# Last state-space unit turned on the vector engine, gated unit first in the fill, modulation loads in the SP queue, a weight tile with a place of its own

## The chip, the cores and the metric

The kernel runs on one core of a Trainium2 chip. The metric is device microseconds (us) from the start to the end of one execution; the median of the runs is compared. The core has five engines that run side by side, each through its own instructions in their order: TensorE (PE in the rows; PEld is its weight load), VectorE (DVE), ScalarE (ACT), GpSimd (POOL) and SyncE (SP). DMA transfers are started by an instruction in the stream of SP or of ACT; such an instruction can wait, for a free buffer for instance, and what stands behind it on that engine then waits too.

## The reference

An encoder trunk with two residual layers, width 1024, 512 tokens, one sequence, all in fp32. The change lies in the first layer, in its mixer:

```python
u = rms_norm(h, norm_w[layer, 0]) * (1.0 + sc1) + sh1
z = u @ hyb_w_in[e]                      # split: state-space part, queries, keys, values
y_s5 = s5_mixer(z_s5, ...)               # 512 wide, forward and backward complex scan
y_att = axial_gqa(z_q, z_k, z_v, ...)    # 512 wide, 8 query heads, 2 key/value heads
mix = jnp.concatenate([y_s5, y_att], axis=-1) @ hyb_w_out[e]
h = h + g1 * mix
# inside s5_mixer, behind the scans:
g = jax.nn.gelu(y)
out = g * jax.nn.sigmoid(g @ glu_w + glu_b)      # the gated unit
```

`sh1, sc1, g1, sh2, sc2, g2` are the modulation: `silu(c) @ ada_w[layer] + ada_b[layer]`, a 1024 x 6144 product for one row. The norm behind the mixer uses `sc2` and `sh2`.

## The kernel before

Matrix products are made in three passes for fp32 accuracy: each operand is split into a high part `hi` (a rounded copy, from ACT or POOL) and a low part `lo` (the difference, from DVE), and `hi*hi + hi*lo + lo*hi` is summed in PSUM. So a weight tile needs a load (`wr`), a cast (`wh`, ACT, line L522) and a subtraction (`wl`, DVE, line L523) before PE can use it whole.

The first layer's mixer runs in this order in the trace. From about 100 us on, the loop in `hybrid` walks eight state-space units (four channel groups, two directions) and lets attention steps run between them. A unit is: a product with the input matrices (L445), a rotation by DVE (L450 to L452) that makes the complex recurrence a real one, two pairs of scans on DVE (L459), and `s5_turn`, which turns the states back: four multiplies (L470 to L473) on the engine that the list `POST` names, two additions on DVE (L475, L476), and the output product on PE (L483). A channel group is finished by `s5_out` (L496 to L503), whose result is a tile of `gts`.

Behind the loop come three things that are interleaved by a scheduler, which orders each engine's instructions by its own estimate, PE's alone being in the order of the code (`manual_schedule`):

- `gelu2` for the four tiles of `gts` (L1109 to L1112), and their split (POOL L520, DVE L523, tile names `actb`);
- the last attention steps (scores L1021 and L1022, row maximum L1024 on DVE, exponential L1028 on ACT, transposes L1036, their copies `pts` L1038, values L1045), and between them the pieces of `fill`. A piece is six matmuls of 128x512: two output tiles, one input tile, three passes. `fill` makes the gated unit (weights `gluw`, inputs `actb`; its exit is a tanh L1143, a product L1144 and a split L1147, L1148 into tiles `ys5`) and half of the output projection: `pa` and `pb`, two tiles each, with weights `wa`, `wb` for the attention half and `ws` for the state-space half;
- `ada_half` for four halves of `sc2` and `sh2`: eight loads of 256 KB each (tile `araw`, line L693), a multiply-add of each into `aacc` on DVE (L695, L700), a transposed copy and a sum (L706, L708), four tiny matmuls (L710, tile `po`).

```python
behind = lambda: self.tc.issue_after(self.scan.ins)
```

keeps `gelu2` and `fill` behind the last scan in the scheduler's order. `hybrid_out` then calls `boundary`, which takes `pa` and `pb` out (L1372 in the profile's numbers) and multiplies the second half of the output projection with four more weight tiles (loads in the SP queue, four buffers of their own).

The tile pools say how many buffers a tile name has: `araw` four, raw weights `wr` three, cast weights `wh`, `wl` two in that stretch; `wa` has its own place in the pool `op`, `wb` has not. A load waits until its buffer's last reader is done.

Of the kernel before, what the change touches and what calls it, by code (L numbers as in the profile page):

```python
# [12 lines left out]
F32R = mybir.dt.float32r  # L13
I32 = mybir.dt.int32
AF = mybir.ActivationFunctionType
# [4 lines left out]
P = 128  # L20
# [40 lines left out]
class Kern:  # L61
# [54 lines left out]
    def setup(self, cols, consts):  # L116
        nc, ctx = self.nc, self.ctx
        G = nc.gpsimd
        self.POST = [(G, G)] * 8
# [258 lines left out]
    def s5_phase(self, sp, pg, d, eng):  # L378


        A = self.nc.scalar
        e = self.tl(sp, "s5e", [P, 12, 128], bufs=2).rearrange("p (i x) j -> p i x j", i=3)
        m4 = self.tl(sp, "s5m4t", [P, 4, 128], bufs=2)
        place = lambda t: t.rearrange("p (a b) j -> p b a j", b=2)
        pairs = lambda t: t.rearrange("p (a b) j -> p a b j", b=2)
        er, ei, ni = (e[:, i, :, d:d + 127] for i in range(3))
        c, s = (t[:, d, pg % 2 * 4:pg % 2 * 4 + 4] for t in self.tabs)
        A.copy(place(er[:, :, 63:127]), pairs(c))
        A.copy(place(ei[:, :, 63:127]), pairs(s))
        A.copy(place(er[:, :, 0:63]), pairs(c[:, :, 63:0:-1]))  # L390
        A.mul(place(ei[:, :, 0:63]), pairs(s[:, :, 63:0:-1]), -1.0)
        A.mul(ni, ei, -1.0)
        x0 = d * 16 + pg * 4
        A.copy(place(m4[:, :, d:d + 127]), pairs(self.s5["m4"][:, x0:x0 + 4].unsqueeze(2).to_broadcast([P, 4, 127])))
        end = slice(127 * (1 - d), 127 * (1 - d) + 1)
        self.nc.gpsimd.memset(m4[:, :, end], 0.0)
        self.nc.gpsimd.memset(e.rearrange("p i x j -> p (i x) j")[:, :, end], 0.0)
        return e, m4
# [28 lines left out]
    def s5_states(self, sp, pg, d, e, m4, ut):  # L427
# [9 lines left out]
        for x1 in range(2):  # L437
# [15 lines left out]
            for i, v in enumerate((vr, vi)):  # L453
# [5 lines left out]
                self.scan = V.tensor_tensor_scan(*z, 0.0, op0=ALU.mult, op1=ALU.add)  # L459
            yield vr, vi  # L460

    def s5_turn(self, pg, d, e, vr, vi, eng):
# [13 lines left out]
        V.tensor_tensor(vr[:, dst], vr[:, dst], vi[:, dst], op=ALU.add)  # L476
# [68 lines left out]
    def wtile(self, src, pool=None):  # L545
# [4 lines left out]
        hi, lo = (self.tl(pool or self.wp, t, [P, self.WC], F32R, bufs=1 if pool else self.WH)[:, 0:n] for t in ("wh", "wl"))  # L550
# [135 lines left out]
    def ada_half(self, aw, l, q, half, tag, eng=None, acc=None, raws=None, trn=None):  # L686
# [4 lines left out]
        for k in range(8):  # L691
            raw = raws()
            self.adma = nc.scalar.dma_start(raw, aw[l, k * 128:(k + 1) * 128, c0:c0 + 512])  # L693
# [420 lines left out]
    def fill(self, op, gts, yatt, acts, gluw, wout, outs):  # L1114
# [14 lines left out]
        pa = [self.psum("p5") for _ in range(2)]  # L1129
        wa = self.wtile(wout[512:1024, 0:256], op)  # L1130
        gw = [self.wtile(gluw[:, 0:256]), self.wtile(gluw[:, 256:512])]
        for a in range(2):
            piece(pa, wa, a, yatt[a], a == 0)
            yield
        for i in range(2):
            ps = [self.psum("pb0"), self.psum("py")]
            for a in range(4):
                piece(ps, gw[i], a, ins[a], a == 0, a == 3)
                yield
            for o in range(2):  # L1140
                g = gts[2 * i + o]
                th = self.tl(op, "gth", [P, 512], bufs=2)
                nc.scalar.activation(th, ps[o], AF.Tanh, bias=self.glubh[:, 2 * i + o:2 * i + o + 1], scale=0.25)  # L1143
# [5 lines left out]
                acts.append((hi, lo))  # L1149
        ws = [self.wtile(wout[0:512, i * 256:i * 256 + 256]) for i in range(2)]  # L1150
        pb = [self.psum("pb0"), self.psum("py")]
# [5 lines left out]
        wb = self.wtile(wout[512:1024, 256:512])  # L1157
# [82 lines left out]
    def hybrid(self, rctx, bctx, xT, aw, win, bc, gluw, wout):  # L1240
# [66 lines left out]
        for i in range(8):  # L1307
# [7 lines left out]
            e = self.s5_phase(lp, pg, d, self.POST[i][0])  # L1315
# [6 lines left out]
            self.s5_turn(pg, d, e[0], *v, self.POST[i][1])(pys[pg])  # L1322
# [23 lines left out]
        behind = lambda: self.tc.issue_after(self.scan.ins)  # L1346
# [15 lines left out]
    def hybrid_out(self, ap2, op, acts, ps, wout, aw):  # L1362
        nc = self.nc
        h = []
        for q, half in self.mods0:
            self.ada_half(aw, 0, q, half, "po", None, lambda: self.tl(op, "aacc", [P, 512], bufs=2),
                          lambda: self.tl(op, "araw", [P, 512], bufs=4), lambda: self.tl(op, "accs", [P, 16], bufs=1))()
# [415 lines left out]
```

## Time and profile before

| | |
|---|---|
| median of three runs | 1242.74 us (1242.69 to 1242.74) |
| the profiled execution | 1244.12 us, of which its span, first to last instruction, is 1242.1 us |
| mean granted TensorE clock | 0.97 of full speed |
| PE busy | 1160.0 us, 93% of the span |
| DVE busy | 792.3 us, 64% |
| ACT busy | 539.1 us, 43% |
| POOL busy | 174.6 us, 14% |
| loads of `araw` in ACT's queue | 32 of 256 KB, 3.0 us from issue to landing (median) |

The busy shares are means over stages with different limits: PE is the busiest engine of the whole, yet in the stretch of this change, 200 to 305 us of the span, it waits several times, and what it waits for has to be read there.

### The profile page before, as it was taken

What the parts mean: (1) busy time and instruction counts of PE and PEld (TensorE: products, weight loads), DVE (VectorE), ACT (ScalarE), POOL (GpSimd) and SP (SyncE); (2) the same over time, 40 slices, a digit from 0 to 9 for tenths busy, and PEclk for the clock granted to TensorE, in tenths of its full rate; (3) what the DMA queues carried; (4) which work ended last, traced back from release to release, by engine and by line L of the source; (5) the groups of instructions that cost most, each with busy time, mean ns of one, the idle gap of its engine ahead of it and who ended that gap; (6) DMA issues with size and microseconds to landing.
All of it is one profiled execution on the core that took longest, in us unless ns stands there. A gap on an engine that the chain in (4) does not pass through costs nothing.

```text
span 1242.1 us, 17018 instructions
## 1 busy us (share of the span) xinstructions
PE 1160.0 (93%) x6584; PEld 974.5 (78%) x6584; DVE 792.3 (64%) x1218; ACT 539.1 (43%) x929; POOL 174.6 (14%) x244
## 2 busy tenths in 40 slices
PE   4898889688999999999999999789999999999997
PEld 3687667567998888888889987569988888888886
DVE  6596988887689975487333799995644333344243
ACT  4366787453444421243322469844433312344230
POOL 2449874300000000000000171000000000000000
PEclk9897999899999999999999999799899999999998
DMA  9421030356258665576322331122233223332311
GB/s 352 153 65 62 21 96 8 121 172 225 77 178 270 231 222 186 174 244 208 102 90 69 127 106 51 51 86 72 80 103 101 102 92 95 102 101 87 101 34 68
DMA packets 85904, 151.75 MB, mean 122 GB/s; under 512 B 5696, under 2 KB 34368, under 8 KB 85824
## 3 DMA queue, kind: packets, MB, share of 16 engines
q1 hardware_dynamic: 81216, 142.28, 35.1%
q10 hardware_dynamic: 4608, 8.39, 2.1%
q8 instruction: 51, 0.84, 0.3%
q14 instruction: 29, 0.24, 0.1%
HBM read 148.55 MB, written 2.10 MB: 121 GB/s over the span
## 4 chain that ended last, share of the span: by engine, by line
PE 73%; DVE 14%; ACT 5%; issue 3%; DMA 3%; POOL 2%; SPq 0%; DVEq 0%; ACTq 0%; POOLq 0%
PE ps L587 13%; PE ps L586 13%; PE ps L588 13%; PE px L586 8%; PE px L588 8%; PE px L587 8%; DMA araw<-ada_w 2%; DVE wl L523 2%; PE p L748 1%; PE pn L855 1%; DVE ti L1530 1%; DVE hs L1529 1%; DVE actb L459 1%; DVE actb L475 1%; DVE actb L905 1%
## 5 line engine op out<-in xcount | busy, mean ns | idle before, releaser
L523 DVE TENSOR_TENSOR wl<-wr,wh 128x1024 fp32r<-128x1024 f32 (+1 forms) x170 | 208.5, 1228 | 273.0 <-ACT wh L522 266.8
L522 ACT CAST wh<-wr 128x1024 fp32r<-128x1024 f32 (+1 forms) x162 | 166.4, 1030 | 416.4 <-PE ps L587 198.4
L587 PE MATMUL ps<-actb,wh 128*128 128x512 f32 (+1 forms) x512 | 181.5, 355 | 0.1
L586 PE MATMUL ps<-acta,wh 128*128 128x512 f32 (+1 forms) x328 | 116.8, 358 | 0.0
L588 PE MATMUL ps<-acta,wl 128*128 128x512 f32 (+1 forms) x328 | 116.3, 355 | 0.0
L586 PE MATMUL ps<-hid,wh 128*128 128x512 f32 x288 | 112.1, 389 | 0.0
L588 PE MATMUL ps<-hid,wl 128*128 128x512 f32 x288 | 112.0, 389 | 0.0
L587 PE MATMUL ps<-hid,wh 128*128 128x512 f32 x288 | 112.0, 389 | 0.0
L587 PEld LDWEIGHTS ps<-actb,wh 128*128 128x128 f32 x512 | 97.9, 191 | 13.5 <-DVE actb L905 0.3
L586 PE MATMUL px<-hid,wh 128*128 128x512 f32 (+1 forms) x288 | 98.9, 343 | 0.0
L587 PE MATMUL px<-hid,wh 128*128 128x512 f32 (+1 forms) x288 | 98.5, 342 | 0.0
L588 PE MATMUL px<-hid,wl 128*128 128x512 f32 (+1 forms) x288 | 98.5, 342 | 0.0
L587 PE MATMUL px<-actb,wh 128*128 128x512 f32 (+1 forms) x224 | 85.5, 382 | 0.0
L668 DVE SCALAR_TENSOR_TENSOR acc<-wr,cact,acc 128x1024 f32<-128x1024 f32 x49 | 62.9, 1283 | 18.8 <-DMA wr<-ada_w 18.3
L586 PEld LDWEIGHTS ps<-acta,wh 128*128 128x128 f32 x328 | 63.1, 192 | 8.4
L588 PEld LDWEIGHTS ps<-acta,wl 128*128 128x128 f32 x328 | 62.9, 192 | 8.5
L586 PE MATMUL ps<-actc,wh 128*128 128x512 f32 (+1 forms) x184 | 65.1, 354 | 0.0
L588 PE MATMUL ps<-actc,wl 128*128 128x512 f32 (+1 forms) x184 | 64.8, 352 | 0.0
L588 PEld LDWEIGHTS ps<-hid,wl 128*128 128x128 f32 x288 | 54.1, 188 | 11.2
L587 PEld LDWEIGHTS ps<-hid,wh 128*128 128x128 f32 x288 | 54.0, 188 | 11.2
L586 PEld LDWEIGHTS ps<-hid,wh 128*128 128x128 f32 x288 | 54.1, 188 | 11.2
L587 PEld LDWEIGHTS px<-hid,wh 128*128 128x128 f32 x288 | 54.6, 190 | 6.3
(504 smaller groups left out, 2593.0 us busy)
## 6 DMA issues: line engine op xcount, KB each, us to landing
wr<-w SPq DMA_DIRECT2D x128, 512.0 KB, 3.7
wr<-ada_w SPq DMA_DIRECT2D x56, 512.0 KB, 4.4
wr<-wout SPq DMA_DIRECT2D x16, 512.0 KB, 3.5
araw<-ada_w ACTq DMA_DIRECT2D x32, 256.0 KB, 3.0
wr<-win SPq DMA_DIRECT2D x16, 512.0 KB, 3.8
wr<-win SPq DMA_DIRECT2D x8, 384.0 KB, 5.9
h<-xT SPq DMA_DIRECT2D x8, 256.0 KB, 5.8
acta<-ada_w SPq DMA_DIRECT2D x8, 256.0 KB, 5.6
```

The costliest lines, as they stand in the source:

```text
L459: self.scan = V.tensor_tensor_scan(*z, 0.0, op0=ALU.mult, op1=ALU.add)
L475: V.tensor_tensor(a[:, dst], a[:, dst], b[:, dst], op=ALU.add)
L522: nc.scalar.copy(hi, src)
L523: (lo_eng or nc.vector).tensor_tensor(lo, src, hi.bitcast(F32), op=ALU.subtract)
L586: mm(out, wh, xh, start=first and a == a0 and lead(o), stop=False, skip_group_check=True)
L587: mm(out, wh, xl, start=False, stop=False, skip_group_check=True)
L588: mm(out, wl, xh, start=False, stop=last and a == a0 + kk - 1, skip_group_check=True)
L668: nc.vector.scalar_tensor_tensor(acc, raw, self.ca[:, k:k + 1], acc, op0=ALU.mult, op1=ALU.add)
L748: self.nc.tensor.matmul(ps[o:o + 32, 0:raws[k].shape[1]], self.ca[:, k:k + 1].to_broadcast([P, 32]), raws[k], start=k < 4, stop=k >= 4, sk ...
L855: nc.tensor.matmul(o[:, t:t + 1], x[:, t * P:t * P + P], self.ones, start=i == 0, stop=i == len(src) - 1)
L905: nc.vector.scalar_tensor_tensor(lo, t, sh[:, k:k + 1], hi.bitcast(F32), op0=ALU.add, op1=ALU.subtract)
L1529: V.tensor_tensor_scan(hs, a[:, 0], ti[:, 0], 0.0, op0=ALU.mult, op1=ALU.add)
```

## The change

The four multiplies of the last unit (`i = 7`) go from POOL to DVE. The scheduler's fence is moved from the last scan to the last addition of the turn. `fill` begins with the gated unit (three of four input tiles for both weight tiles, then the fourth for both), and the first two attention pieces of `pa` come behind it; the PSUM banks are handed out accordingly. `wb` gets a place of its own in `op` and its load and cast come before `ws`. The 32 loads of `ada_half` are issued by SP in place of ACT, into six buffers in place of four.

```diff
-        self.POST = [(G, G)] * 8
+        self.POST = [G] * 7 + [nc.vector]
...
         V = self.nc.vector
         V.tensor_tensor(a[:, dst], a[:, dst], b[:, dst], op=ALU.add)
-        V.tensor_tensor(vr[:, dst], vr[:, dst], vi[:, dst], op=ALU.add)
+        self.turned = V.tensor_tensor(vr[:, dst], vr[:, dst], vi[:, dst], op=ALU.add)
...
-    def wtile(self, src, pool=None):
+    def wtile(self, src, pool=None, tag=""):
...
-        hi, lo = (self.tl(pool or self.wp, t, [P, self.WC], F32R, bufs=1 if pool else self.WH)[:, 0:n] for t in ("wh", "wl"))
+        hi, lo = (self.tl(pool or self.wp, t + tag, [P, self.WC], F32R, bufs=1 if pool else self.WH)[:, 0:n] for t in ("wh", "wl"))
...
-            self.adma = nc.scalar.dma_start(raw, aw[l, k * 128:(k + 1) * 128, c0:c0 + 512])
+            nc.sync.dma_start(raw, aw[l, k * 128:(k + 1) * 128, c0:c0 + 512])
...
-        pa = [self.psum("p5") for _ in range(2)]
+        gw = [self.wtile(gluw[:, 0:256]), self.wtile(gluw[:, 256:512])]
         wa = self.wtile(wout[512:1024, 0:256], op)
-        gw = [self.wtile(gluw[:, 0:256]), self.wtile(gluw[:, 256:512])]
-        for a in range(2):
-            piece(pa, wa, a, yatt[a], a == 0)
+        pg = []
+        for i in range(2):
+            pg.append([self.psum(("pb0", "py")[i]), self.psum("p5")])
+            for a in range(3):
+                piece(pg[i], gw[i], a, ins[a], a == 0)
+                yield
+        for i in range(2):
+            piece(pg[i], gw[i], 3, ins[3], last=True)
             yield
-        for i in range(2):
-            ps = [self.psum("pb0"), self.psum("py")]
-            for a in range(4):
-                piece(ps, gw[i], a, ins[a], a == 0, a == 3)
-                yield
             for o in range(2):
                 g = gts[2 * i + o]
                 th = self.tl(op, "gth", [P, 512], bufs=2)
-                nc.scalar.activation(th, ps[o], AF.Tanh, bias=self.glubh[:, 2 * i + o:2 * i + o + 1], scale=0.25)
+                nc.scalar.activation(th, pg[i][o], AF.Tanh, bias=self.glubh[:, 2 * i + o:2 * i + o + 1], scale=0.25)
...
                 acts.append((hi, lo))
+        pa = [self.psum("pb0"), self.psum("p5")]
+        for a in range(2):
+            piece(pa, wa, a, yatt[a], a == 0)
+            yield
+        wb = self.wtile(wout[512:1024, 256:512], op, "b")
         ws = [self.wtile(wout[0:512, i * 256:i * 256 + 256]) for i in range(2)]
-        pb = [self.psum("pb0"), self.psum("py")]
+        pb = [self.psum("py"), self.psum("p5")]
...
-        wb = self.wtile(wout[512:1024, 256:512])
         piece(pa, wa, 2, yatt[2])
...
-            self.s5_turn(pg, d, e[0], *v, self.POST[i][1])(pys[pg])
+            self.s5_turn(pg, d, e[0], *v, self.POST[i])(pys[pg])
...
-        behind = lambda: self.tc.issue_after(self.scan.ins)
+        behind = lambda: self.tc.issue_after(self.turned.ins)
...
-                          lambda: self.tl(op, "araw", [P, 512], bufs=4), lambda: self.tl(op, "accs", [P, 16], bufs=1))()
+                          lambda: self.tl(op, "araw", [P, 512], bufs=6), lambda: self.tl(op, "accs", [P, 16], bufs=1))()
```

The order of the instructions moves at these places. First DVE behind the scans of the last unit (L459; `actb` are the unit's states and the split gelu tiles, `wl` the low halves of weight tiles, `esum` a row maximum). Before:

```order
L459 SCALAR_TENSOR_TENSOR actb_565_2689<-s5m4t_564_2680,p5_569_2708 128x255
L459 SCALAR_TENSOR_TENSOR actb_566_2690<-s5m4t_564_2680,p5_569_2708 128x255
L1110 SCALAR_TENSOR_TENSOR nt_583_2775<-nt_583_2775,h_260_1354 128x512
L1110 SCALAR_TENSOR_TENSOR nt_584_2780<-nt_584_2780,h_356_1761 128x512
L523 TENSOR_TENSOR wl_606_2837<-wr_604_2835,wh_605_2836 128x1024
L523 TENSOR_TENSOR wl_609_2843<-wr_607_2841,wh_608_2842 128x1024
L1024 TENSOR_REDUCE esum_239_1180<-pa0_541_2566 128x1
L1112 SCALAR_TENSOR_TENSOR h_260_1354<-nt_583_2775,h_260_1354 128x512
L475 TENSOR_TENSOR actb_571_2723<-actb_571_2723,actb_572_2724 128x511
L1112 SCALAR_TENSOR_TENSOR h_356_1761<-nt_584_2780,h_356_1761 128x512
L476 TENSOR_TENSOR actb_565_2689<-actb_565_2689,actb_566_2690 128x511
L523 TENSOR_TENSOR actb_592_2812<-h_260_1354,actb_591_2811 128x512
```

and now:

```order
L459 SCALAR_TENSOR_TENSOR actb_565_2689<-s5m4t_564_2680,p5_569_2708 128x255
L459 SCALAR_TENSOR_TENSOR actb_566_2690<-s5m4t_564_2680,p5_569_2708 128x255
L470 TENSOR_TENSOR actb_571_2723<-s5e_563_2679,actb_565_2689 128x511
L472 TENSOR_TENSOR actb_572_2724<-s5e_563_2679,actb_566_2690 128x511
L471 TENSOR_TENSOR actb_565_2689<-s5e_563_2679,actb_565_2689 128x511
L473 TENSOR_TENSOR actb_566_2690<-s5e_563_2679,actb_566_2690 128x511
L475 TENSOR_TENSOR actb_571_2723<-actb_571_2723,actb_572_2724 128x511
L1024 TENSOR_REDUCE esum_239_1180<-pa0_541_2566 128x1
L476 TENSOR_TENSOR actb_565_2689<-actb_565_2689,actb_566_2690 128x511
L1110 SCALAR_TENSOR_TENSOR nt_583_2775<-nt_583_2775,h_260_1354 128x512
L1110 SCALAR_TENSOR_TENSOR nt_584_2780<-nt_584_2780,h_356_1761 128x512
L523 TENSOR_TENSOR wl_601_2829<-wr_599_2827,wh_600_2828 128x1024
```

Four multiplies stand in front of L475, and both additions L475 and L476 have moved ahead of the gelu (L1110) and of the two weight tiles (L523).

Second, ACT where the loads were (L693 `araw`; L498 and L503 copies of `s5_out`, L522 casts of weight tiles). Before:

```order
L498 COPY s5g_573_2746<-py_558_2647 128x512
L503 COPY h_549_2602<-p5_574_2748 128x512
L522 CAST wh_602_2830<-wr_601_2829 128x1024
L693 DMA araw_687_3260<-ada_w 128x512
L1109 ACTIVATE nt_586_2790<-h_549_2602 128x512
L693 DMA araw_688_3263<-ada_w 128x512
L693 DMA araw_689_3266<-ada_w 128x512
L693 DMA araw_690_3269<-ada_w 128x512
L1111 ACTIVATE nt_586_2790<-nt_586_2790 128x512
L693 DMA araw_691_3272<-ada_w 128x512
L693 DMA araw_692_3275<-ada_w 128x512
L693 DMA araw_693_3278<-ada_w 128x512
```

and now, at the same copies:

```order
L498 COPY s5g_573_2746<-py_558_2647 128x512
L1038 COPY pts_590_2809<-pt_589_2804 128x512
L1109 ACTIVATE nt_585_2785<-h_468_2236 128x512
L503 COPY h_549_2602<-p5_574_2748 128x512
L522 CAST wh_606_2840<-wr_605_2839 128x1024
L522 CAST whb_668_3116<-wr_667_3115 128x1024
L1027 ACTIVATE esum_239_1180<-esum_239_1180,rqy_237_1171 128x1
L1109 ACTIVATE nt_586_2790<-h_549_2602 128x512
L1111 ACTIVATE nt_585_2785<-nt_585_2785 128x512
L1028 ACTIVATE pexp_588_2801,esum_239_1180<-pa1_587_2797,esum_239_1180,rqy_237_1171 128x512
```

The loads are gone from ACT, and the cast of `wb` (`whb`) has come to stand right behind that of `wa`.

Third, SP around the weights of the second half of the output projection (`wr_747` to `wr_756`). Before:

```order
L553 DMA wr_750_3466<-wout0 128x2x512
L553 DMA wr_753_3496<-wout0 128x2x512
L553 DMA wr_756_3526<-wout0 128x2x512
L553 DMA wr_799_3774<-w1 128x2x512
L553 DMA wr_802_3804<-w1 128x2x512
L553 DMA wr_809_3850<-w1 128x2x512
L1345 DMA xs_580_2764<-xT 128x512
L1345 DMA xs_581_2765<-xT 128x512
```

and now:

```order
L553 DMA wr_750_3466<-wout0 128x2x512
L693 DMA araw_728_3384<-ada_w 128x512
L553 DMA wr_753_3496<-wout0 128x2x512
L693 DMA araw_729_3387<-ada_w 128x512
L693 DMA araw_730_3390<-ada_w 128x512
L553 DMA wr_756_3526<-wout0 128x2x512
L553 DMA wr_799_3774<-w1 128x2x512
L553 DMA wr_802_3804<-w1 128x2x512
L553 DMA wr_809_3850<-w1 128x2x512
L1349 DMA xs_580_2764<-xT 128x512
L1349 DMA xs_581_2765<-xT 128x512
```

Those four tiles stand between the last loads of the modulation, the first of them behind the 29th of 32.

## Rows read from the trace of the kernel before

**Rows 1.** Windows: us, then busy us of PE, PEld, DVE, ACT, POOL; PEclk; DMA.

```profile
199.50:225.80 26.30, 23.23 (x222) 17.96 (x220) 25.05 (x41) 17.55 (x40) 10.58 (x17) 1.00 0.01 1
225.80:244.00 18.20, 9.60 (x62) 7.63 (x60) 15.70 (x19) 9.55 (x20) 9.05 (x7) 0.81 0.42 134
244.00:305.30 61.30, 54.27 (x312) 41.19 (x312) 49.09 (x73) 29.40 (x57) 0.62 (x1) 0.94 0.59 193
305.30:345.00 39.70, 39.60 (x346) 38.96 (x346) 27.69 (x68) 17.16 (x36) 0.00 (x0) 1.00 0.32 106
```

**Rows 2.** Timeline of DVE, 224 to 246 us: start, length, what, idle before.

```profile
224.56 1.26 DVE L459 TENSOR_TENSOR_SCAN actb<-s5m4t,p 128x255 f32<-128x255 f32 x2
225.74 3.17 DVE L1110 SCALAR_TENSOR_TENSOR nt<-nt,h 128x512 f32<-128x512 f32 x2
228.84 4.49 DVE L523 TENSOR_TENSOR wl<-wr,wh 128x1024 fp32r<-128x1024 f32 x2
233.25 0.68 DVE L1024 TENSOR_REDUCE esum<-pa 128x1 f32<-128x512 f32 x1
233.85 0.68 DVE L1112 SCALAR_TENSOR_TENSOR h<-nt,h 128x512 f32<-128x512 f32 x1
234.46 0.68 DVE L475 TENSOR_TENSOR actb<-actb,actb 128x511 f32<-128x511 f32 x1
...
243.99 1.23 DVE L523 TENSOR_TENSOR wl<-wr,wh 128x1024 fp32r<-128x1024 f32 x1 [1.49 <-ACT wh L522]
245.13 0.69 DVE L1110 SCALAR_TENSOR_TENSOR nt<-nt,h 128x512 f32<-128x512 f32 x1
```

**Rows 3.** Timeline of POOL: first and last of its four multiplies.

```profile
225.41 1.28 POOL L470 TENSOR_TENSOR actb<-s5e,actb 128x511 f32<-128x511 f32 x1 [7.06 <-DVE actb L459]
...
230.01 2.24 POOL L473 TENSOR_TENSOR actb<-s5e,actb 128x511 f32<-128x511 f32 x1
```

**Rows 4.** Timeline of PE, 235 to 305 us: its waits, and its last.

```profile
235.19 2.07 PE L483 MATMUL py<-s5c,actb 128*128 128x128 f32 x8 [5.08 <-DVE actb L475]
...
244.01 0.51 PE L586 MATMUL p<-acta,wh 128*128 128x512 f32 x1 [1.62 <-ACT wh L522]
...
267.76 0.50 PE L1021 MATMUL pa<-kth,q 128*128 128x512 f32 x1 [1.70 <-ACT pexp L1028]
...
297.35 0.80 PE L588 MATMUL pb<-acta,wl 128*128 128x512 f32 x1 [3.15 <-DVE wl L523]
...
305.02 0.39 PE L588 MATMUL py<-acta,wl 128*128 128x512 f32 x1
```

**Rows 5.** DVE from 225.8 to 303.5 us: windows, then groups by line.

```profile
225.80:303.50 77.70, 62.07 (x367) 47.57 (x366) 62.99 (x88) 38.23 (x74) 9.67 (x8) 0.91 0.55 179
...
L700 DVE SCALAR_TENSOR_TENSOR aacc<-araw,cact,aacc 128x512 f32<-128x512 f32 x27 | 20.7, 766 | 9.2 <-DMA araw<-ada_w 8.6
```

**Rows 6.** Waits from 225.8 to 305.5 us: total, times, longest.

```profile
DVE aacc L700 <- DMA araw<-ada_w: 8.6, 8, 2.6
PE pa L1021 <- ACT pexp L1028: 3.3, 3, 1.7
DVE aacc L695 <- DMA araw<-ada_w: 1.2, 1, 1.2
```

**Rows 7.** Timeline of ACT and its DMA queue, 246 to 302 us.

```profile
246.25 4.30 ACTq L693 DMA_DIRECT2D araw<-ada_w  x4
250.59 0.59 ACT L1038 COPY pts<-pt 128x512 f32<-128x512 f32 x1 [4.11 <-DMA araw<-ada_w]
...
298.37 3.90 ACT L522 CAST wh<-wr 128x1024 fp32r<-128x1024 f32 x4 [6.52 <-DVE mod L718]
```

**Rows 8.** Timeline of SP's DMA queue, 233 to 290 us.

```profile
233.87 4.31 SPq L1345 DMA_DIRECT2D xs<-xT  x5
245.24 43.93 SPq L553 DMA_DIRECT2D wr<-wout  x5
```

**Rows 9.** The loads' tile araw: issue to landing.

```profile
DMA to landing us min/median/max: 2.7/3.0/5.6
```

More of the change, by code (lines that the diff above doesn't have):

```diff
@@ L376, in s5_prep, with s5_phase @@
         yield
-    def s5_phase(self, sp, pg, d, eng):
+    def s5_phase(self, sp, pg, d):
         A = self.nc.scalar
@@ L458, in s5_states @@
                     z = vx[:, 254::-1], mx[:, 255:0:-1], q[:, i, 255:0:-1]
-                self.scan = V.tensor_tensor_scan(*z, 0.0, op0=ALU.mult, op1=ALU.add)
+                V.tensor_tensor_scan(*z, 0.0, op0=ALU.mult, op1=ALU.add)
             yield vr, vi
@@ L1314, in hybrid @@
                 gts.append(self.tl(self.hp, "h", [P, 512], bufs=9))
-            e = self.s5_phase(lp, pg, d, self.POST[i][0])
+            e = self.s5_phase(lp, pg, d)
             if i == 3:
```

## The prediction

> **What bounds the kernel now.** I read the windows first, to see which engine is full where the change lies. PE is the busiest engine of the kernel, but not here. From 199.5 to 225.8 us DVE works 25.05 of 26.3 us; from 225.8 to 244.0 PE works 9.60 of 18.2 at a granted clock of 0.81; from 244.0 to 305.3 it works 54.27 of 61.3 at 0.94; only from 305.3 on is it full, 39.60 of 39.7 at full clock [rows 1]. So a gain before 305.3 us moves all that follows, and none is to be had behind it.
>
> Then the timelines. PE waits 5.08 us for L475, the first addition of the last turn [rows 4]. L475 starts at 234.46, 8.7 us after the scans end at 225.74 [rows 2], because POOL multiplies from 225.41 to 232.25 [rows 3] and because the scheduler had put gelu and weight tiles ahead of it. The fill's first matmul starts at 244.01, after a wait for a cast [rows 4] that stands on ACT behind the copies of the last state-space output. Its last starts at 305.02 [rows 4].
>
> Inside that stretch the waits name the loads of the modulation: DVE waits 8.6 + 1.2 us for `araw` [rows 6]. ACT, which issues them, is held by them: after four issues that took 4.30 us its next copy had waited 4.11 us, and casts at 298.37 had waited 6.52 us [rows 7]. PE's wait of 3.15 us at 297.35 for `wl` of `wb` [rows 4] comes from the same place: that subtraction stands in DVE's order behind multiplies that waited for loads.
>
> **The turn on DVE.** It adds four multiplies of 128x511 to DVE. The trace has none of L470 there; the nearest rows are an operation of that size and kind and its neighbours, which start 0.60 us apart (233.25, 233.85, 234.46) [rows 2]: 2.4 us. It takes POOL's four away. While they ran, two L1110 took 3.10 us from start to start and two weight tiles 4.41 us; alone, a tile takes 1.14 (243.99 to 245.13) and a 512-wide operation 0.60 [rows 2], so DVE lost 1.90 + 2.13 = 4.0 us to POOL. The net on DVE is -1.6 us.
>
> That the loss is POOL's doing, the rows show only by coincidence in time. The Trainium skill, page "SBUF — State Buffer", section "Who interferes with whom", says that a VectorE instruction with two SBUF inputs contends with a GpSimd instruction that reads SBUF, and that the later one blocks. Both slow kinds have two such inputs. By that rule the 4.0 us come back in full; without it they might not, and DVE's end below would be 4.0 us later, at 290.2 plus its idle time.
>
> **The start of the fill.** DVE's order up to the scans hardly changes, so I keep 225.74 as the anchor (give or take 1 us for rows that swapped). Then four multiplies, 2.4; L475, 0.6: 228.7 in place of 235.1. One row maximum and L476: 229.9. Two L1110, 1.2, two weight tiles, 2.3, two L1112, 1.2, a maximum, 0.6, and the low half of the first gelu tile, 0.6: 235.8. With a matmul's start after that: about 236.4. The first piece now is one of the gated unit, which needs this tile and weights that are split by 233.4, and no longer the cast that it waited for at 244.01. So the fill starts **7.6 us earlier**.
>
> **From there to the fill's end.** The number of matmuls is the same. PE took 61.3 us: 54.27 busy, 7.0 idle. At a clock of 0.94, 6% of the busy time, 3.3 us, was lost to the half clock, so the work is 51.0 us at full clock [rows 1]. The floor is 236.4 + 51.0 = 287.4.
>
> What stays on top, from the idle time of before:
> - The wait for `wb` (3.15) goes: its own place lets it be cast and split before the loads' multiplies, as the order on ACT shows. The waits at the start (0.5 more inside the stretch) go with the cast.
> - The waits for the exponentials, 3.3 us [rows 6], hang on row maxima that queue on DVE among the multiplies. With DVE still full I keep half: 1.7.
> - Two new ones. The third gelu tile is split only at about 243.2 by DVE's order, PE can be there at about 242.1: 1.1. And the exit of the gated unit (four times L1144 and L1148, with two weight tiles between them) now comes at once, hidden by only two pieces of `pa` and some attention; the last row maximum stands among it, at about 268.2, and the transpose that needs it waits about 1.2.
> - The half clock followed the idle stretches (0.81 between 225.8 and 244.0); PE's longest wait goes, so I keep 0.6 of the 3.3.
>
> Sum: 287.4 + 1.7 + 1.1 + 1.2 + 0.6 = **292.0**, in place of 305.3: a gain of 13.3 us.
>
> **Does DVE allow that?** From 225.8 to 303.5 it was busy 63.0 us of 77.7 [rows 5]. Now 63.0 + 2.4 - 4.0 - 1.0 (a sum and two small operations that moved behind) = 60.4, so it could reach the same point at 286.2, if it never idled. Its idle time was 14.7, of it 9.8 for loads.
>
> The loads now start behind five loads of `xs`, which took 0.86 us each [rows 8]: about 239, against 242.44 on ACT, and 256 KB then land every 0.86 us. A transposed copy keeps a buffer until its sum is made, and in DVE's order, before and now, the second and third sums (L708) stand behind the last weight tiles of the stretch: before, that left 2 of 4 buffers for the last eight loads, now 4 of 6. A buffer's round is 3.0 us of landing [rows 9], 0.67 us of multiply (mean 766 ns less the overlap of successive ones) [rows 5] and some 0.3 of issue: a load every 2.0 us with two buffers, every 1.0 with four. So I leave 3 to 4 us of idle time: DVE ends at about 290, just ahead of PE.
>
> **The queue that the loads move into.** In SP's order the four weight tiles of the second half stand behind the 29th load. Before, the last of them was issued by 289.2 [rows 8]. Now the first goes out when DVE has multiplied some 25 loads, by the steps above at about 278; with landing, cast and split it is ready near 285, before PE asks for it at 292. I cost this at nothing; the cover is 7 us. ACT gets its 4 and 6.5 us stops back, but it is not full (29.40 of 61.3 us [rows 1]), so they count only through the casts named above.
>
> Behind 305.3 the order of the instructions is the same but for a few rows of the second layer, which I set to zero.
>
> **The rivals.**
> - *No idle time is left*: the floor of 287.4, a gain of 17.9 us, 1224.8. For it: ACT and its casts are free of loads. Against: DVE is full, and every row maximum queues on it.
> - *The gated unit's exit becomes the wait*: the eight DVE operations lag, and PE stands before the first `ys5` piece. Each microsecond that DVE is behind costs one; at 4 us more the fill ends at 296, 1233.4.
> - *The loads still pace DVE*, from SP as from ACT: with the old idle time, 14.7 us, DVE ends at 225.8 + 60.4 + 14.7 = 300.9, a gain of 4.4 us, 1238.3. For it: the loads' round is no shorter. Against: half again as many buffers. This is also the case in which the move of the loads doesn't do what it says.
> - *SP's order holds the weight tiles back* (slower): if the loads fall behind so far that the 29th goes out after 298.5, the first tile, 7 us later, is ready only past 305.5, and PE stands at the start of the second half. At 302 it would cost 3.5 us: 1246. Even at the pace of before (the multiplies ran from 245.7 to about 305) the 25th multiply falls near 280, so this needs a new stall. The page "DMA: Bandwidth & Descriptors" of the Trainium skill, section "Queues, rings and completion order", says that each DMA engine takes turns between queues; by that rule tiles and loads in one queue lose the turns that they had in two, which speaks for this rival. No run here shows it.
>
> **The numbers.** Forecast (fill's end 288.5 to 295) 0.60; no idle left 0.10; late exit 0.12; loads still pacing 0.13; tiles held back 0.05. The profiled execution took 1244.12 us, 1.4 above the median: 1230.8 for such a one, and **1229.4** for the median, 1242.74 - 13.3. The range, 1222.5 to 1238.5, holds the first four cases; the forecast's own is 1226 to 1233. I take 0.2%, 2.5 us, as what a measurement can tell from no change. Faster 0.91: the first four, less 0.04 for the case in which the loads pace and the half clock stays. Same 0.05, slower 0.04.
>
> **What would show it.** L475 starting near 229; two L1110 at 0.60 us each; the first gated-unit matmul near 236; no ACT wait for `araw`; PE's wait before the `wb` pieces gone; DVE's wait for `araw` near 3 us; the second half starting near 292 and then full to the same length. It is wrong if PE waits at the first `ys5` piece or at `wh_748`, if the clock stays at its lower level past 240, or if the scans themselves end later than 226.

## The result and the profile after

The changed kernel takes 1230.26 us (median of four runs, 1228.0 to 1232.16) where the one before took 1242.74 beside it: a ratio of 0.9897, 95% interval 0.9876 to 0.9918. Run again with the experiments below it took 1228.15 us, ratio 0.9871 (0.9856 to 0.9885). The forecast was 1229.4, the range 1222.5 to 1238.5. The profiled execution took 1232.16 us with a span of 1230.4.

First the windows of the changed kernel, cut where the old stages were cut: the turn, the start of the fill, the fill, the second half of the projection. The columns are those of [rows 1].

```profile
225.80:235.90 10.10, 8.53 (x77) 6.96 (x73) 10.10 (x17) 7.00 (x16) 1.07 (x2) 1.00 0.16 54
235.90:244.00 8.10, 6.96 (x34) 4.75 (x34) 7.25 (x12) 5.89 (x12) 1.12 (x2) 0.79 0.96 330
244.00:293.90 49.90, 46.58 (x270) 36.55 (x270) 43.55 (x65) 25.11 (x50) 0.72 (x1) 0.97 0.64 216
293.90:333.60 39.70, 39.60 (x350) 38.73 (x350) 29.54 (x71) 18.16 (x38) 0.00 (x0) 1.00 0.35 113
```

The last stage is as full as it was, 39.60 us of PE in 39.7 at full clock [rows 1]; it begins at 294 in place of 305.3. What went is ahead of it.

DVE's timeline at the turn, against [rows 2]:

```profile
225.22 1.26 DVE L459 TENSOR_TENSOR_SCAN actb<-s5m4t,p 128x255 f32<-128x255 f32 x2
226.39 0.67 DVE L470 TENSOR_TENSOR actb<-s5e,actb 128x511 f32<-128x511 f32 x1
...
228.17 0.69 DVE L473 TENSOR_TENSOR actb<-s5e,actb 128x511 f32<-128x511 f32 x1
228.77 0.69 DVE L475 TENSOR_TENSOR actb<-actb,actb 128x511 f32<-128x511 f32 x1
229.37 0.69 DVE L1024 TENSOR_REDUCE esum<-pa 128x1 f32<-128x512 f32 x1
229.97 0.69 DVE L476 TENSOR_TENSOR actb<-actb,actb 128x511 f32<-128x511 f32 x1
230.57 1.30 DVE L1110 SCALAR_TENSOR_TENSOR nt<-nt,h 128x512 f32<-128x512 f32 x2
231.78 2.36 DVE L523 TENSOR_TENSOR wl<-wr,wh 128x1024 fp32r<-128x1024 f32 x2
234.05 1.30 DVE L1112 SCALAR_TENSOR_TENSOR h<-nt,h 128x512 f32<-128x512 f32 x2
```

The multiplies start 0.6 us apart, L475 at 228.77, and with POOL silent two L1110 take 1.21 us from start to start and two weight tiles 2.27.

PE's first matmul of the fill and its waits of more than half a microsecond up to the fill's end, against [rows 4]:

```profile
235.88 0.50 PE L586 MATMUL pb<-actb,wh 128*128 128x512 f32 x1 [1.00 <-POOL actb L520]
237.00 0.50 PE L587 MATMUL pb<-actb,wh 128*128 128x512 f32 x1 [0.62 <-DVE actb L523]
...
244.38 0.50 PE L1021 MATMUL pa<-kth,q 128*128 128x512 f32 x1 [0.90 <-ACT pexp L1028]
...
258.94 0.50 PE L1021 MATMUL pa<-kth,q 128*128 128x512 f32 x1 [0.84 <-ACT pexp L1028]
...
267.13 0.50 PE L1021 MATMUL pa<-kth,q 128*128 128x512 f32 x1 [2.10 <-ACT pexp L1028]
```

No wait for L475, for a weight tile's cast or for the low half of `wb` is left: 1.62 us for the first gelu tile at the fill's start, then exponentials alone. Three of the grouped waits from 225 to 296 us, in total, times and longest, against [rows 6]:

```profile
ACT wh L522 <- DMA wr<-wout: 8.0, 4, 4.2
PE pa L1021 <- ACT pexp L1028: 3.8, 3, 2.1
DVE aacc L700 <- DMA araw<-ada_w: 0.8, 1, 0.8
```

DVE waits 0.8 us for the loads of the modulation, ACT not at all. The loads that ACT waits for now are the four weight tiles of the second half, and SP's timeline shows why:

```profile
241.71 40.85 SPq L693 DMA_DIRECT2D araw<-ada_w  x25
282.60 0.94 SPq L553 DMA_DIRECT2D wr<-wout  x2
283.88 0.34 SPq L693 DMA_DIRECT2D araw<-ada_w  x1
284.26 0.43 SPq L553 DMA_DIRECT2D wr<-wout  x1
```

They go out from 282.60 on, behind the loads. PE asks for the first at 294 and doesn't wait.

### The profile page after: what moved, and what is told of

It reads as the page before. It is cut to its first block, busy times and chain, and to the rows that moved or that the text cites. A ratio compares the mean times of both kernels' runs of the same rounds, so it can differ in the third digit from the quotient of the medians.

```text
span 1230.4 us, 17016 instructions
## 1 busy us (share of the span) xinstructions
PE 1156.2 (94%) x6584; PEld 970.9 (79%) x6584; DVE 790.8 (64%) x1223; ACT 538.9 (44%) x929; POOL 167.3 (14%) x239
## 4 chain that ended last, share of the span: by engine, by line
PE 75%; DVE 14%; ACT 5%; issue 2%; POOL 2%; DMA 1%; SPq 0%; DVEq 0%; POOLq 0%; ACTq 0%
PE ps L587 13%; PE ps L588 13%; PE ps L586 13%; PE px L586 8%; PE px L588 8%; PE px L587 8%; DVE wl L523 2%; PE p L748 1%; PE po L1045 1%; DVE ti L1534 1%; DVE actb L459 1%; DVE hs L1533 1%; ACT pexp L1028 1%; PE p L587 1%; PE p L586 1%
## 5 line engine op out<-in xcount | busy, mean ns | idle before, releaser
L523 DVE TENSOR_TENSOR wl<-wr,wh 128x1024 fp32r<-128x1024 f32 (+1 forms) x169 | 205.1, 1215 | 272.5 <-ACT wh L522 265.7
L522 ACT CAST wh<-wr 128x1024 fp32r<-128x1024 f32 (+1 forms) x161 | 165.8, 1030 | 419.9 <-PE ps L587 200.4
```

The costliest lines, as they stand in the source:

```text
L522: nc.scalar.copy(hi, src)
L523: (lo_eng or nc.vector).tensor_tensor(lo, src, hi.bitcast(F32), op=ALU.subtract)
```

## The experiments

The twelve ran in four sets (e1 to e4, e5 to e8, e9 to e11, e12), each beside runs of the kernel before, whose medians were 1243.58, 1243.58, 1243.77 and 1244.32 us. One execution of a kernel differs from the next by some microseconds already ahead of this change's place, so the profiles are compared from the last scans' start, S (the last pair of L459 on DVE). L475, F (the first 128x512 matmul of the fill) and E (the first 128x256 matmul of the second half) are given as their start less S. The clock's loss is PE's busy time from F to E times one less the granted clock there, from a window of F to E; its two digits make it good to some 0.3 us. Each row of the table is one profiled execution, but for the medians. E of the kernel before and of the changed one:

```profile
305.51 0.39 PE L586 MATMUL pa<-acta,wh 128*128 128x256 f32 x1
294.20 0.39 PE L586 MATMUL pa<-acta,wh 128*128 128x256 f32 x1
```

| kernel | median us | ratio to before (95%) | S | L475 | F | E | clock's loss |
|---|---|---|---|---|---|---|---|
| before | 1242.74 | | 224.56 | 9.90 | 19.45 | 80.95 | 3.3 |
| changed | 1230.26 | 0.9897 (0.9876 to 0.9918) | 225.22 | 3.55 | 10.66 | 68.98 | 3.2 |
| e9, changed again | 1228.15 | 0.9871 (0.9856 to 0.9885) | 221.09 | 3.56 | 10.65 | 68.05 | 1.6 |
| e1, turn and fence alone | 1232.95 | 0.9915 (0.9899 to 0.9931) | 223.42 | 4.16 | 11.26 | 70.47 | 1.6 |
| e5, fence alone | 1231.98 | 0.9903 (0.9890 to 0.9915) | 223.55 | 3.40 | 12.04 | 70.45 | 3.2 |
| e8, all but turn and fence | 1235.26 | 0.9925 (0.9911 to 0.9939) | 219.29 | 9.89 | 15.89 | 72.67 | 1.6 |
| e2, turn back on POOL | 1232.41 | 0.9912 (0.9897 to 0.9928) | 222.68 | 3.40 | 12.79 | 71.10 | 3.2 |
| e6, fence back on the scan | 1229.50 | 0.9891 (0.9877 to 0.9906) | 223.56 | 9.30 | 10.12 | 68.77 | 0 |
| e7, old order of the fill | 1229.81 | 0.9889 (0.9876 to 0.9902) | 224.84 | 4.16 | 11.26 | 67.08 | 1.6 |
| e3, loads in ACT's queue | 1231.75 | 0.9910 (0.9893 to 0.9928) | 223.09 | 3.56 | 10.65 | 71.05 | 1.6 |
| e4, four buffers | 1229.38 | 0.9891 (0.9873 to 0.9910) | 221.19 | 3.55 | 10.65 | 68.36 | 1.6 |
| e11, `wb` shares again | 1227.60 | 0.9863 (0.9838 to 0.9888) | 222.93 | 3.56 | 10.65 | 65.88 | 0 |
| e10, matmuls in two waits | 1227.86 | 0.9868 (0.9853 to 0.9883) | 223.18 | 3.56 | 10.88 | 66.53 | 0 |
| e12, third order of the fill | 1228.79 | 0.9884 (0.9865 to 0.9903) | 222.32 | 3.56 | 10.65 | 66.39 | 0 |

**e1, the turn and the fence alone**, in the kernel before:

```diff
-        self.POST = [(G, G)] * 8
+        self.POST = [(G, G)] * 7 + [(G, nc.vector)]
...
-        V.tensor_tensor(vr[:, dst], vr[:, dst], vi[:, dst], op=ALU.add)
+        self.turned = V.tensor_tensor(vr[:, dst], vr[:, dst], vi[:, dst], op=ALU.add)
...
-        behind = lambda: self.tc.issue_after(self.scan.ins)
+        behind = lambda: self.tc.issue_after(self.turned.ins)
```

> The kernel before with one edit of the change alone: the last unit's four multiplies on DVE, with the scheduler's fence moved to the turn's last addition. By my sum the turn brings L475 from 234.46 to about 229 us, PE's wait of 5.08 us for it goes and the two L1110 and two weight tiles beside it take 1.2 and 2.3 us in place of 3.10 and 4.41. But the loads stay in ACT's queue with four buffers, and they paced DVE (8.6 + 1.2 us of waits), so by my theory only a part of the 7.6 us at the start reaches the end: 1237 to 1240 us. Rival: the turn is the whole change and the loads were hidden anyway; then 1230 to 1234. Second rival: the turn is worth only what DVE gains net, 1.6 us: 1241.

1232.95 us: the first rival. Two edits out of five bring 10.6 us, with the loads in ACT's queue and in four buffers. Those were not what held the end: E came 10.5 us closer to S without them, more than the 7.6 us that I had given to the start.

**e2, the turn back on POOL**, in the changed kernel:

```diff
-        self.POST = [G] * 7 + [nc.vector]
+        self.POST = [G] * 8
```

> The changed kernel with the last unit's four multiplies back on POOL and nothing else undone. By my theory the start of the fill goes back by some 6 us (first fill matmul near 242 in place of 235.88), L1110 takes about 1.5 us each again, and a little of it is caught up in PE's waits for exponentials: 1235 to 1238 us. Rival: the start does not matter, because DVE is the bound of the stretch and gains only 1.6 us net from the turn: 1231 to 1232.

1232.41 us, just above the rival's 1231 to 1232 and below my theory's 1235 to 1238. The start did not go back by 6 us but by 2.1 (F from 10.66 to 12.79), and L475 stayed at 3.40 behind S. So with the fence on the turn the engine of the multiplies does not delay L475, which led to e5 and e6.

**e3, the loads in ACT's queue**, still six buffers:

```diff
-            nc.sync.dma_start(raw, aw[l, k * 128:(k + 1) * 128, c0:c0 + 512])
+            nc.scalar.dma_start(raw, aw[l, k * 128:(k + 1) * 128, c0:c0 + 512])
```

> The changed kernel with the 32 loads of ada_half issued by ACT again, still into six buffers. By my theory ACT is then held by loads that wait for buffers, as before (4.11 and 6.52 us), but less with six buffers; casts and exponentials behind them come late and PE's waits for exponentials grow by 1 to 4 us: 1231 to 1234 us. Rival: with six buffers the queue makes no difference, since SP's own order delays the weight tiles as much: 1228 to 1230.5. Rival: the queue was the main gain: above 1235.

As the theory had it: 1231.75 us, E 2.1 us later than in the changed kernel's profile and 3.0 later than in e9. ACT stood 7.8 us for buffers, and PE's waits for exponentials grew from 3.8 to 7.4 us. The intervals of e3 and of the changed kernel's first runs overlap, those of e3 and e9 don't.

**e4, four buffers**:

```diff
-                          lambda: self.tl(op, "araw", [P, 512], bufs=6), lambda: self.tl(op, "accs", [P, 16], bufs=1))()
+                          lambda: self.tl(op, "araw", [P, 512], bufs=4), lambda: self.tl(op, "accs", [P, 16], bufs=1))()
```

> The changed kernel with four buffers of araw in place of six, loads still in SP's queue. By my theory the last eight loads then have two free buffers in place of four, DVE waits for araw some 8 us more than the 0.8 us of now, and the four weight tiles of the second half, which stand behind the 29th load in SP's queue, go out that much later than 282.60 us: PE, which asks for the first at 294, waits 2 to 6 us: 1232 to 1237 us. Rival: the slack holds and the buffers bring nothing: 1228 to 1231.

The rival: 1229.38 us. DVE does wait more, 5.0 + 0.8 us for `araw` in place of 0.8, and nothing comes of it.

**e5, the fence alone**: of e1's diff the last two edits, the multiplies left on POOL.

> The kernel before with the scheduler's fence alone moved from the last scan to the turn's last addition; the four multiplies stay on POOL. New theory: what moved L475 forward is its place in DVE's order, ahead of the gelu and weight-tile work, and POOL's multiplies, with DVE quiet beside them, shrink from 6.84 to about 5 us; the engine of the multiplies matters little. Then L475 starts some 3.5 us after the last scans' start in place of 9.9, the fill some 12 to 13 us after it in place of 19.45, and the kernel takes 8 to 11 us less than before. Rival (my prediction's step): the turn's engine makes the gain; with POOL still at it, at most 2 to 4 us less than before.

1231.98 us, 11.6 less than before, where 8 to 11 were expected. The scheduler's fence alone, without any work moved between engines, gives most of the 12.5 to 15.6 us of the whole change. POOL's and DVE's timelines in that kernel, and the fill's first matmul on PE:

```profile
224.41 1.28 POOL L470 TENSOR_TENSOR actb<-s5e,actb 128x511 f32<-128x511 f32 x1 [7.06 <-DVE actb L459]
225.64 1.28 POOL L472 TENSOR_TENSOR actb<-s5e,actb 128x511 f32<-128x511 f32 x1
226.85 1.29 POOL L471 TENSOR_TENSOR actb<-s5e,actb 128x511 f32<-128x511 f32 x1
228.09 1.73 POOL L473 TENSOR_TENSOR actb<-s5e,actb 128x511 f32<-128x511 f32 x1
```

```profile
225.46 0.69 DVE L1024 TENSOR_REDUCE esum<-pa 128x1 f32<-128x512 f32 x1 [0.65 <-PE pa L1022]
226.95 1.74 DVE L475 TENSOR_TENSOR actb<-actb,actb 128x511 f32<-128x511 f32 x1 [0.80 <-POOL actb L472]
229.84 0.69 DVE L476 TENSOR_TENSOR actb<-actb,actb 128x511 f32<-128x511 f32 x1 [1.16 <-POOL actb L473]
```

```profile
235.59 0.50 PE L586 MATMUL p<-acta,wh 128*128 128x512 f32 x1 [1.62 <-ACT wh L522]
```

With the gelu and the weight tiles held back, DVE has a row maximum to do and then waits, and POOL's four multiplies are through in 5.4 us (224.41 to 229.82) in place of 6.84 [rows 3]. L475 no longer stands behind other work. Where L475 and a multiply of POOL run side by side, both are slow: 1.74 us for L475, which takes 0.69 in the changed kernel, and 1.73 for L473 in place of 1.28.

**e6, the fence back on the scan**, the multiplies on DVE:

```diff
-                V.tensor_tensor_scan(*z, 0.0, op0=ALU.mult, op1=ALU.add)
+                self.scan = V.tensor_tensor_scan(*z, 0.0, op0=ALU.mult, op1=ALU.add)
...
-        behind = lambda: self.tc.issue_after(self.turned.ins)
+        behind = lambda: self.tc.issue_after(self.scan.ins)
```

> The changed kernel with the fence back on the last scan and the multiplies on DVE. The scheduler then puts two L1110 and two weight tiles ahead of the turn and spreads the turn among gelu work: from the row order L475 starts about 9 us after the last scans' start. New theory (the place in the order counts): PE waits some 4 us at the turn's product and 8 to 11 us less than before remain, 2 to 4 less gain than the whole change. Rival (the engine counts): no difference from the whole change, 12 to 13 us less than before.

1229.50 us, 14.1 less than before and no more than the whole change takes: the rival. L475 is late again, 9.30 us behind S, as my theory had it, and yet nothing is lost. PE stands 3.10 us for an exponential and 0.48 at the turn's product, and then has its fill. PE's timeline there:

```profile
232.76 0.50 PE L1021 MATMUL pa<-kth,q 128*128 128x512 f32 x1 [3.10 <-ACT pexp L1028]
...
233.68 0.47 PE L586 MATMUL pb<-actb,wh 128*128 128x512 f32 x1
233.99 1.05 PE L483 MATMUL py<-s5c,actb 128*128 128x128 f32 x8
234.80 0.47 PE L587 MATMUL pb<-actb,wh 128*128 128x512 f32 x1
```

The gelu work is done first, so that the gated unit begins 10.12 us behind S, ahead of the turn's product (L483) and mixed with it. With the multiplies on DVE, either the turn or the first gelu tiles can go first there. What that owes to the engine, e8 shows below.

**e7, the old order of the fill**: the two attention pieces of `pa` first again, then the gated unit, `wb` (own place) and `ws`; all else as changed.

```diff
+        pa = [self.psum("p5") for _ in range(2)]
+        wa = self.wtile(wout[512:1024, 0:256], op)
         gw = [self.wtile(gluw[:, 0:256]), self.wtile(gluw[:, 256:512])]
-        wa = self.wtile(wout[512:1024, 0:256], op)
-        pg = []
+        for a in range(2):
+            piece(pa, wa, a, yatt[a], a == 0)
+            yield
...
```

> The changed kernel with the pieces of the fill in the order of before: the two attention pieces of pa first, then the gated unit, and the second half of wout behind the two state-space weight tiles; its own place for that tile, the turn, the fence and SP's queue stay. By my steps the fill's start then waits for the cast and the split of the first weight tile, which cost 1.6 + 1.5 us of PE's time where only the turn was changed: 1 to 3 us slower than the whole change, 10 to 12 less than before. Rival: the order makes no difference, since PE loses 1.6 us there in either order: within 1 us of the whole change.

The rival, 1229.81 us: as fast as the whole change. The 1.62 + 1.52 us that PE waits for the first weight tile are there, as expected, but its waits for exponentials shrink to 0.38, 1.25 and 0.37 us. The new order takes from one place and gives at another.

**e8, all but the turn and the fence**: e6's diff and `self.POST = [G] * 8` in the changed kernel.

> The changed kernel with both the multiplies back on POOL and the fence back on the last scan, so that only the order of the fill, the SP queue, the six buffers and the tile's own place are changed. New theory (gains overlap): the start stays late (L475 nearly 10 us after the last scans' start), but the first gated-unit pieces can run around the wait and the loads no longer hold ACT: 5 to 9 us less than before. Rival (the parts simply add: fence and turn alone gave 10.6 of 12.5 us): 2 us less than before.

1235.26 us, 8.3 less than before, inside the theory's 5 to 9. But no piece of the fill runs around the wait: PE waits for L475 again, and the turn's product, which takes 3.41 us (1.95 in the changed kernel's profile), stands ahead of the fill's first matmul:

```profile
229.95 3.41 PE L483 MATMUL py<-s5c,actb 128*128 128x128 f32 x16 [3.44 <-DVE actb L475]
```

In E, the fence alone gives 10.5 us, the rest alone 8.3, all together 12.0 (12.9 in e9): the parts overlap by more than 5 us.

e8 and e6 differ in the engine of the multiplies and in nothing else. DVE behind the scans, two rows of e8 (POOL multiplies beside it), then two of e6:

```profile
220.47 3.17 DVE L1110 SCALAR_TENSOR_TENSOR nt<-nt,h 128x512 f32<-128x512 f32 x2
223.56 4.49 DVE L523 TENSOR_TENSOR wl<-wr,wh 128x1024 fp32r<-128x1024 f32 x2
224.74 1.27 DVE L1110 SCALAR_TENSOR_TENSOR nt<-nt,h 128x512 f32<-128x512 f32 x2
225.93 2.35 DVE L523 TENSOR_TENSOR wl<-wr,wh 128x1024 fp32r<-128x1024 f32 x2
```

The same four operations take 7.58 us in e8, from the first's start to the last's end, and 3.54 in e6. With the fence on the scan, then, the engine counts: F is 15.89 against 10.12, and the medians of this one set 1235.26 against 1229.50. With the fence on the turn it counts for little: e2 lost 2.1 us in F and 2 to 4 in the median, and e5 is no slower than e1.

**e9, the changed kernel again**, no edit.

> The changed kernel as it is, once more, beside the two runs below: 1228 to 1232 us, 11 to 14 us less than before, with the last scans starting anywhere from 221 to 226 us and the second half of the projection 68.5 to 69.5 us behind them.

1228.15 us, 15.6 less than before in that set, and E at 68.05: more gain than the 14 us, and nearer than the 68.5, that I had allowed.

**e10, matmuls in PE's waits**, in the changed kernel:

```diff
...
+        def warm(ps, n):
+            y = yatt[0][0]
+            for _ in range(n):
+                nc.tensor.matmul(ps, y[:, 0:P], y, start=True, stop=True)
...
+                if i == 0 and a == 0:
+                    with self.tc.issue_after(self.outt.ins):
+                        warm(pg[0][0], 6)
...
+            if a == 0:
+                warm(pb[0], 8)
...
```

> The changed kernel with 14 more matmuls of 128x512 on PE, whose results are overwritten: 6 in its wait before the fill's first matmul and 8 in its wait of 2.1 us for an exponential; DVE, ACT and SP keep their order. It does extra work. Theory (the half clock follows PE's idle stretches, and that is the term I sized at 0.6 and measured at some 3 us): the granted clock stays at 1.00 behind both places, the second half of the projection starts 2 to 3 us closer to the last scans' start than 68.98, and the time is 2 to 3 us less than the changed kernel's. Rival (the clock falls whatever PE does in those waits): clock near 0.6 again at the same places, 0 to 1 us more than the changed kernel.

In the profile the clock is as the theory had it: windows of the changed kernel at its half clock, and of this one behind the same two places.

```profile
238.00:242.00 4.00, 4.00 (x25) 2.85 (x25) 3.93 (x6) 1.96 (x5) 0.22 (x1) 0.60 1.01 356
268.70:272.20 3.50, 3.50 (x21) 2.49 (x19) 3.45 (x8) 1.93 (x5) 0.00 (x0) 0.54 0.38 128
```

```profile
234.06:240.00 5.94, 5.32 (x35) 3.53 (x33) 5.94 (x8) 4.98 (x9) 0.57 (x2) 1.00 0.96 327
264.20:270.00 5.80, 5.80 (x40) 4.64 (x41) 5.76 (x11) 2.86 (x6) 0.00 (x0) 1.00 0.33 94
```

E is 66.53, 2.4 us nearer than in the changed kernel's profile, 1.5 nearer than in e9's. The times don't show it: 1227.86 against 1228.15 in the same set.

**e11, `wb` in the shared buffers**, loaded behind the state-space pieces again:

```diff
-        wb = self.wtile(wout[512:1024, 256:512], op, "b")
...
+        wb = self.wtile(wout[512:1024, 256:512])
         piece(pa, wa, 2, yatt[2])
```

> The changed kernel without the place of its own for the second half of wout: it shares the two buffers of the other weight tiles again and is loaded behind the state-space pieces. My prediction gave its wait 3.15 us. New theory (that wait came from DVE being late, and an early start of the fill took it away by itself: with the turn alone 0.35 us were left): within 1 us of the changed kernel, with PE's wait for wl there under 1 us. Rival (the prediction's term): 2 to 3 us more than the changed kernel.

The new theory: 1227.60 us, and no wait of PE for `wl` at that place. It also weakens e10: PE waited 2.09 us for the same exponential, and in this execution the clock stayed at 1.00 behind it, without any added matmul. So e10 does not show that its matmuls kept the clock up.

**e12, a third order of the fill**, to part the two exits of the gated unit:

```diff
-        pg = []
+        pa = [self.psum("p5") for _ in range(2)]
         for i in range(2):
-            pg.append([self.psum(("pb0", "py")[i]), self.psum("p5")])
-            for a in range(3):
-                piece(pg[i], gw[i], a, ins[a], a == 0)
+            ps = [self.psum("pb0"), self.psum("py")]
+            for a in range(4):
+                if a == 3 * (1 - i):
+                    piece(pa, wa, i, yatt[i], i == 0)
+                    yield
+                piece(ps, gw[i], a, ins[a], a == 0, a == 3)
                 yield
...
```

> The changed kernel with a third order of the fill: it begins with three pieces of the gated unit, as the change does, but the two attention pieces of pa stand between the pieces of the gated unit's first weight tile and around its exit, so that the two exits (tanh, product, split) come apart in time and not together. Theory (what is left above PE's own work are ACT's exponentials queued behind both exits at once, 2.1 us at the longest wait, and the half clock behind that wait): fill's start 10.65 us behind the last scans' start as now, the second half of the projection 65 to 67 us behind it in place of 68 to 69, and the time 1 to 3 us under the changed kernel's, near 1227. Rival (the waits for exponentials only move to other rows): 68 to 69 us, and the changed kernel's time.

E came to 66.39, in the expected stretch, but with no clock lost, as in e11, whose order of the fill is the changed kernel's; its waits for exponentials were 1.57, 1.78 and 0.37 us, 3.7 in all, like the changed kernel's 3.8. So the waits moved, as the rival had it, and the time, 1228.79 us, is the changed kernel's. None of the versions is shown to beat it.

## Why the prediction was right, and where it was right for the wrong reason

Counted from S, the prediction put E near 67.6 (292.0 + 0.2 - 224.56, the 0.2 being the step from 305.3 to E's 305.51); it was 68.98, and 68.05 in e9. The gain of 13.3 us came out as 12.0 and 12.9 at E, and as 12.5 and 15.6 in the medians of the two sets. Of the 12.0, 8.8 are the earlier start, 2.6 less idle time of PE from F to E (4.5 us for 7.0) and 0.6 less work there.

- **The turn on DVE.** Each duration held: multiplies 0.6 us apart, L1110 at 0.60, a weight tile at 1.14. L475 starts 3.55 us behind S, and the sum has it start 3.6 behind (225.74 + 2.4 - 224.56; its 228.7 is L475's end). That the 4.0 us were lost to POOL is now shown by e8 and e6 (7.58 us for 3.54) and not by coincidence alone. The Trainium skill, page "SBUF — State Buffer", section "Who interferes with whom", says that a VectorE instruction with two SBUF inputs contends with a GpSimd one that reads SBUF. The trace agrees, and in e5 the loss falls on both (1.74 for 0.69, 1.73 for 1.28).
- **The start of the fill: right number, half the cause.** 10.66 us behind S, 11.8 predicted; the sum waited for the low half of the first gelu tile, and the first matmul needs the high half alone (POOL L520). I gave the gain to the engine. The runs show two edits that can stand in for each other: with the multiplies on POOL and only the fence moved, F falls from 19.45 to 12.04, and moving the multiplies as well takes 0.8 more (e5, e1); with the fence left on the scan, moving the multiplies takes F from 15.89 to 10.12 (e8, e6). The one starts the gelu work behind POOL's multiplies, the other takes these off POOL. I had named the gelu work ahead of L475 as a second cause, but made the sum on DVE's new order as a whole and did not price the two apart. What the engine alone does in the kernel before, whose fill begins with the attention pieces, was not run.
- **The wait for `wb`: right number, another cause.** The 3.15 us went, but a place of its own was not needed: with the old place they are gone too (e11), with turn and fence alone 0.35 were left (e1), with the fence alone none (e5). An early start is enough, then. In e8, whose fill starts 5.2 us later than the changed kernel's, they are gone as well, so the place or the free queue may do it too; which, was not tried.
- **The waits for exponentials.** 1.7 + 1.2 predicted, 3.8 measured. The row maximum was not the whole of the last one; ACT's own queue was, full with the exits of the gated unit:

```profile
264.28 0.71 ACT L1143 ACTIVATE gth<-p,glubh 128x512 f32<-128x512 f32 x1
264.85 0.61 ACT L1038 COPY pts<-pt 128x512 f32<-128x512 f32 x1
265.32 0.68 ACT L1147 ACTIVATE ys<-h 128x512 fp32r<-128x512 f32 x1
265.85 0.33 ACT L1027 ACTIVATE esum<-esum,rqy 128x1 f32<-128x1 f32 x1
266.21 0.78 ACT L1028 ACTIVATE pexp<-pa,esum,rqy 128x512 f32<-128x512 f32 x1
```

  PE stood from 265.03; between these rows ACT has no gap. I wrote that ACT is not full and counts only through casts, from a share of the whole stretch. The 1.1 us for the third gelu tile did not come; 0.62 behind F for the low half of the first one did.
- **The half clock: the term that was mis-sized.** 0.6 us predicted, 3.2 lost in the profiled execution, 1.6 in e9's, none in e11's and e12's. I took PE's longest wait, which went, as its cause. The clock fell behind shorter ones too: it was 0.60 from 238 to 242 us, behind waits of 1.00 and 0.62, and 0.54 from 268.7 to 272.2, behind one of 2.10. What decides it stays open (last section). So one sign that I had named for being wrong did show, the lower level past 240 us, and a second by a little: the scans ended at 226.5, S being 0.7 later. The fill ended 68.8 us behind S (294.02), 67.4 forecast. That is 2.6 more for the clock and 0.5 more idle time (58.32 - 53.86 = 4.5 from F to E, 4.0 forecast), less 1.2 for the start and 0.4 for the work (50.6, 51.0 forecast): together 1.5, against the 1.4 that it came late.
- **The loads.** I left DVE 3 to 4 us of waiting for them; it was 0.8. ACT's freedom was worth 2 to 3 us in the profiles (e3). The six buffers were worth nothing that could be measured (e4), and the rival in which the loads pace DVE never came near.
- **SP's queue.** Costing it at nothing was right; the slack was some 5 us and not 7. The first tile went out at 282.60 (278 forecast), was split by 289.0 (285) and wanted at 294.2 (292). The 25th multiply, behind which it goes out, I had put too early: near 280 at the pace of before, where its row stands at 285.45. With the turn on POOL (e2) ACT stood 8.5 us before the first of these tiles, DVE 5.1 us for its cast, and PE 0.6 us in the second half for a sum (L708) that stands behind it on DVE. That is much like the slower rival's chain, at a price of 0.6 us.

What stays open: how much of the 12 to 15 us in the medians is ahead of S. The kernel before has one profile, with S at 224.56; the others lie from 219.3 to 225.2, the changed kernel's own two 4.1 us apart.

## What to carry to other kernels

When a wait has two causes in a row, the engine's speed and the place in another engine's order, price both by themselves: here moving a scheduler's fence, with no work moved, brought 11.6 us where the whole change brings 12.5 to 15.6. Gains at one bottleneck overlap. What is lost when one part alone is undone can be nothing (the buffers, the tile's own place, the order of the fill), but two parts can stand in for each other, so undo them together too: the fence undone lost nothing (e6), the multiplies 2 to 4 us (e2), both 5 to 7 (e8). Compare stretches from a common event near the change, not from the start of the span.

## What was not expected of the hardware

The half clock of PE (the lower of its two levels, 1.2 and 2.4 GHz) is not a property of the program alone. In seven profiles PE waited 2.08 to 2.10 us before the same matmul, for the same exponential. Behind that wait the granted clock fell in four of them (the changed kernel, e2, e4, e9) and stayed at 1.00 in three (e3, e6, e11). Windows behind it in e9, which is the changed kernel again, and in e11, which differs in the place and the load of `wb` alone:

```profile
263.00:267.10 4.10, 4.10 (x25) 2.98 (x23) 4.05 (x9) 2.29 (x5) 0.00 (x0) 0.58 0.44 131
262.90:268.00 5.10, 5.10 (x37) 4.07 (x38) 5.05 (x11) 2.84 (x6) 0.00 (x0) 1.00 0.35 104
```

At the fill's start the clock fell in the changed kernel's first profile and not in e9, the same program. Each fall cost some 1.6 us (3.5 us at 0.54, for one). Ahead of S it differs too: from 100 to 219 us the mean granted clock was 0.90 in the changed kernel's profile and 0.93 in e9's. Whether that makes their 4.1 us there was not tried, and what makes the clock fall in one execution and not in another stays open. The runs of the changed kernel lie from 1226.49 to 1232.16 us, so a difference of 2 us can't be read from one execution.
